# First pair's tokens turned by their gather, final norm weights by products, another order in the tail: a decoder layer on one core

## The chip, the cores and the metric

The kernel runs on one core of a Trainium2 chip. Its engines run side by side and meet at semaphores: PE (TensorE, matrix products into PSUM; PEld is its weight load), DVE (VectorE), ACT (ScalarE), POOL (GpSimd) and SP (SyncE, which here issues transfers to the 16 DMA engines). The metric is the device time of one execution in microseconds (us). Before the change, three runs gave 929.28 to 930.95 us with a median of 929.9 us.

## The reference, cut to what matters

One decoder layer on 512 tokens of 1024 numbers, in float32: a mixer of two kinds of attention, a residual, a two-level mixture of 32 experts, a residual, a final norm.

```python
def rms_norm(x, g):
    y = xf * lax.rsqrt(jnp.mean(xf * xf, axis=-1, keepdims=True) + EPS)
    return (y * g).astype(x.dtype)
...
    combine = jnp.einsum('tk,tke->te', w, jax.nn.one_hot(expert_id, MOE_N_EXPERTS, dtype=f32))
    for e in range(MOE_N_EXPERTS):
        hdn = jax.nn.silu(vt @ w_gate[e]) * (vt @ w_up[e])
        y = y + (combine[:, e:e + 1].astype(hdn.dtype) * hdn) @ w_down[e]
...
        h = h + hybrid_mixer(u, positions, w_in[layer], ...)
        h = h + hier_moe(rms_norm(h, g_ffn[layer]), w_grp[layer], b_grp[layer], w_exp[layer], b_exp[layer],
                         w_gate[layer], w_up[layer], w_down[layer])
    return rms_norm(h, g_final)
```

Each token goes to two of the 32 experts. An expert has three matrices of 2 MB each, so that all experts together hold 201 MB of weights, and all of them are read.

## The kernel before

The first half of the program (to about 447 us) is the mixer. Then comes the routing, and from about 452 us the experts, in 16 pairs. An expert has room for 64 of its tokens, so a pair fills 128 rows (a branch behind L1610 deals with experts that got more).

**The expert loop (L1407).** For each pair the rows of its tokens are gathered (`gather_rows`, an indirect DMA from `hs`, the copy of the layer's rows in DRAM), turned by eight transposes on PE into one PSUM tile named `y` (`turn_rows`, L1341), and scaled by the norm's gain into `xa` or `xb` (`turned`, L1346). `up_proj` (L1434) multiplies them with the gate weights (tile `g`) and the up weights (tile `u`), in eight steps k of 128 input columns. SiLU and a product with `u` follow (tile `pkM`, L1463 and L1465), four transposes (L1474), the down products into `y` (L1489), the scaling by the router's weight as a high and a low part (`scaled`, L1394 and L1395), and `combine` (L1389, L1390): one-hot products that scatter the pair's rows back to the tokens, and additions into `h`. `combine` of a pair runs between the gate and up products of the next one, in two halves of 512 columns.

**The weight ring (L1056 to L1076).** 22 tiles of 1 MB hold weights that are loaded ahead. `weights()` takes pieces in order; `refill()` starts as many loads as pieces were used up. In `up_proj` that is after the fourth and after the eighth step k, two pieces of 1 MB each. SP issues the loads in program order, and at most eight are under way.

**The first pair.** It does not gather by DMA, since its rows are still in `h`. `first_rows` multiplies the one-hot matrix `oh` (128 slots) with `h` (L1354, eight products of 512 columns, in float32) to get the rows, `rows_in` holds them, and `turn_rows` turns them. `oh` is built by DVE in `one_hot` (L1309), and right behind it DVE computes the remaining ranks (L1304) and their maximum `cmax` (L1318). Then `slots_of` finds the slots' weights and indices (L1365, `cw`, `idx`), and `gather_rows(1)` fetches the next pair's rows.

**The tail (L1502 on).** The last pair's down products are made in three column groups, `TAIL` = 512, 256 and 256 columns (`down`, L1531). Each group is scaled (`high` on ACT, `low` on DVE), scattered (`spread_out`, L1550: for each of four token tiles the high product, then the low one), added to `h` (`add_of`, L1557), and the squares of the sums are taken (`square`, L1561, in halves of 512 columns). `scale_of` makes 1/rms on POOL (L1521, L1522), `scaled_out` multiplies and stores (L1565 to L1567). `gfin`, the final norm's gain repeated over 128 partitions, is loaded by DMA (L1441).

**What sets the order.** On PE, SP, ACT and DVE the loop's order is that of the code, mostly (`manual_schedule`); before the loop a scheduler decides. The framework places the waits: for a PSUM tile it tracks the tile as a whole.

Of the kernel before, what the change touches and what calls it, by code (L numbers as in the profile page):

```python
# [11 lines left out]
F32 = mybir.dt.float32  # L12
# [9 lines left out]
P = 128  # L22
T = 512
# [24 lines left out]
def _w_in_columns():  # L48
# [13 lines left out]
_PACKS = {  # L62
    "E": [("gmix", 8), ("ident", 128), ("slot", 64), ("gff8", 8), ("none", 8), ("invf", 32), ("rowmask", 2), ("posv", 16), ("posk", 16),
# [19 lines left out]
def build(tc, A, dbg=None):  # L83
# [1222 lines left out]
    def one_hot(quad):  # L1306
        oh = wst.tile([P, NT, 4, CAP], F32R, name="raw2")
        for t in range(NT):
            tt(oh[:, t], slot[:, None, :].to_broadcast([P, 4, CAP]),  # L1309
               val[:, t, 4 * quad:4 * quad + 4][:, :, None].to_broadcast([P, 4, CAP]), op=OP.is_equal)  # L1310
        return oh
# [32 lines left out]
    def turned(pair, tp):  # L1344
        for ks in ((slice(0, 4), slice(4, 8)) if pair == 0 else (slice(0, 8),)):
            nc.vector.tensor_tensor(xs[pair][:, ks], tp[:, ks], cst("gff8")[:, ks, None].to_broadcast([P, ks.stop - ks.start, P]), op=OP.mult)  # L1346

    def first_rows():

        for half in range(2):  # L1350
            cs = slice(half * 512, half * 512 + 512)
            ps = pp.tile([P, 512], F32, name="cT"[half], bufs=2)
            for t in range(NT):
                mm(ps, fl2(oh[:, t, :2]).bitcast(F32), h[t][:, cs], start=t == 0, stop=t == NT - 1)  # L1354
            if half == 0:
                nc.scalar.activation(rows_in[:, cs], ps, AF.Copy)
            else:
                nc.vector.tensor_copy(rows_in[:, 512:768], ps[:, :256])
                nc.scalar.activation(rows_in[:, 768:], ps[:, 256:], AF.Copy)

# [40 lines left out]
    acc = h  # L1401
    rows_in = wst.tile([P, D], F32, name="raw0")
    before = None
    slots, xs = {}, {}
    ab, halves = {}, {}
    loads.enter_context(tc.manual_schedule(engines={E.PE}))
    for pair in range(NE // 2):  # L1407
        last = pair == NE // 2 - 1

        def rest_of(pcw, py, pyh, pair=pair, last=last):  # L1410

            combine(pyh, 0)
# [10 lines left out]
            spread(pair)  # L1423

# [13 lines left out]
        order = ExitStack()  # L1438
        if pair == NE // 2 - 2:
            gfin = wst.tile([P, D], F32, name="raw2")  # L1440
            nc.sync.dma_start(gfin, A["gfin"])  # L1441
        if pair == 0:
            order.enter_context(tc.manual_schedule(engines={E.Activation, E.DVE}))
        if pair == 0:
            first_rows()
            turned(0, turn_rows(0))
            slots_of(0)
            slots_of(1)
            gather_rows(1)
            for tag, k in [("g", k) for k in range(0, KD, 2)] + [("u", k) for k in range(0, KD, 2)]:  # L1450
                up_proj(tag, (k, k + 1))
                if (tag, k) == ("u", 4):
# [9 lines left out]
        sl = wk.tile([P, FF], F32, name="pkM")  # L1462
        nc.scalar.activation(sl, ab[pair, "g"], AF.Silu, scale=cw[:, 1:2])  # L1463
        if not last:
            tt(sl, sl, ab[pair, "u"], op=OP.mult)  # L1465
            up_proj("g", range(4), pair + 1)
        else:
            for _ in between:
                pass
            order.close()  # L1470
        if not last:
            tp = pp.tile([P, 4, P], F32, name="T", bufs=2)
# [29 lines left out]
        else:  # L1502
            hdT = wk.tile([P, 4, P], F32, name="xb")
            for j in range(4):
                tt(sl[:, j::4], sl[:, j::4], ab[pair, "u"][:, j::4], op=OP.mult)
                tp = pp.tile([P, P], F32, name="Tc"[j % 2], bufs=2)
                nc.tensor.transpose(tp, sl[:, j::4], ident)
                if j % 2:
                    nc.scalar.activation(hdT[:, j], tp, AF.Copy)
                else:  # L1510
                    nc.vector.tensor_copy(hdT[:, j], tp)

            ss3 = wk.tile([P, NT, 3], F32, name="ss3")
            nc.vector.memset(ss3[:, :, 1:2], EPS)
# [4 lines left out]
            def scale_of(t):  # L1519
                ts = slice(t, t + 1)  # L1520
                nc.gpsimd.tensor_tensor(rs3[:, 0, ts], rs3[:, 0, ts], ss3[:, t, 2:], op=OP.add)  # L1521
                nc.gpsimd.tensor_tensor(rs3[:, 1, ts], rs3[:, 0, ts], nhalf[:, ts], op=OP.pow)  # L1522
                return rs3[:, 1, ts]
# [17 lines left out]
            def spread_out(i, tags, per):  # L1541

                c0, n = TAIL[i]
                o = slice(c0 % 512, c0 % 512 + n)
                out = []
                for t in range(NT):
                    if t % per == 0:
                        ps = pp.tile([P, per, n], F32, name=tags[t], **({} if tags[t] in "guy" else dict(bufs=2)))
                    for v, y in enumerate((yhi, ylo)):
                        mm(ps[:, t % per], ohs[:, t].bitcast(y.dtype), y[:, o], start=v == t % per == 0,  # L1550
                           stop=v == 1 and t % per == per - 1, skip_group_check=True)
                    out.append(ps[:, t % per])
# [6 lines left out]
            def square(t, half):  # L1559
                jk = wk.tile([P, 512], F32, name="pkM")  # L1560
                nc.scalar.activation(jk, acc[t][:, 512 * half:512 * half + 512], AF.Square, scale=ROOT,  # L1561
                                     accum_out=ss3[:, t, 2 * half:2 * half + 1])

# [4 lines left out]

            loads.enter_context(tc.manual_schedule(engines={E.Activation, E.DVE}))
            high, low = down(0)  # L1570
# [39 lines left out]
    with tc.If(nmax > CAP):  # L1610
# [44 lines left out]
        for t in range(NT):  # L1655
            nc.vector.tensor_tensor(gh[t], acc[t], gfin, op=OP.mult)
            nc.scalar.activation(acc[t], acc[t], AF.Square, scale=ROOT, accum_out=ss3[:, t, 2:])
# [7 lines left out]
def pack(inputs):  # L1665
# [37 lines left out]
    put("gff8", f("g_ffn")[0].reshape(P, KD))  # L1703
    put("gffT", f("g_ffn")[0].reshape(KD, P).T)
    put("br", np.repeat(np.concatenate([f("b_grp")[0], f("b_exp")[0]])[None], P, 0))
    i = np.arange(P)
# [22 lines left out]
    for n in ("w_gate", "w_up", "w_down"):  # L1729
        d[n] = f(n)[0]  # L1730
    d["gfin"] = np.repeat(f("g_final")[None], P, 0)
    return d
# [13 lines left out]
```

## Time and profile before

| | us |
|---|---|
| median of three runs | 929.9 (929.28 to 930.95) |
| the profiled execution | 930.93 |
| its span, first to last instruction | 929.1 |
| around the span | 1.8 |

| engine | busy, us | share of the span |
|---|---|---|
| PE | 890.2 | 96% |
| PEld | 569.5 | 61% |
| DVE | 469.0 | 50% |
| ACT | 252.6 | 27% |
| POOL | 99.4 | 11% |

PE's share is an average over stages with different limits. From 500 to 890 us the DMA engines are full as well, and it is the waits at the end of that stretch, and what ran dry at its start, that tell which of the two sets the time. The mean granted clock was 0.988 of full speed.

### The profile page before, as it was taken

To read this page: it belongs to the slowest core of one execution; us is meant where nothing else is said; L and a number is where in the kernel's file an instruction comes from. 1 tells how busy PE (TensorE), PEld (TensorE's weight loads), DVE (VectorE), ACT (ScalarE), POOL (GpSimd) and SP (SyncE) were. 2 spreads that over 40 slices of the span, in tenths; PEclk is the share of its full clock that TensorE was granted. 3 is DMA by queue.
4 is the path that set the end of the run, shared out by engine and by line. 5 is a ranking of instruction groups with operands and counts; after the bars stand their busy time and mean duration, and the time that the engine had idled before them with its cause. 6 is when DMAs were issued, how large, how long until landed. Compare 5 with 4: busy or idle time off the path is not lost. (4 is left out here: it accounts for less than half of the span.)

```text
span 929.1 us, 12699 instructions
## 1 busy us (share of the span) xinstructions
PE 890.2 (96%) x4908; PEld 569.5 (61%) x4908; DVE 469.0 (50%) x1047; ACT 252.6 (27%) x539; POOL 99.4 (11%) x139
## 2 busy tenths in 40 slices
PE   8997999999999999999899999999999999999994
PEld 5877997899878777899534443444444334333432
DVE  5669664485877776644514433334343324322334
ACT  6542443245545555343101011001011100010014
POOL 0304000032111121500100000000000000000003
PEclk9997999999999999999999999999999999999997
DMA  8821222212111121995889999999999999999992
GB/s 320 315 90 46 91 86 65 77 54 66 49 46 46 47 80 53 416 419 188 317 357 419 419 418 420 419 419 420 419 418 420 419 418 421 418 420 418 421 381 109
DMA packets 47712, 251.89 MB, mean 271 GB/s; under 512 B 6114, under 2 KB 9442, under 8 KB 22688
## 3 DMA queue, kind: packets, MB, share of 16 engines
q1 hardware_dynamic: 45488, 247.10, 66.8%
q0 software_dynamic: 2160, 3.93, 1.1%
q8 instruction: 41, 0.67, 0.3%
q14 instruction: 23, 0.19, 0.1%
HBM read 250.23 MB, written 4.19 MB: 274 GB/s over the span
## 5 line engine op out<-in xcount | busy, mean ns | idle before, releaser
L1390 DVE TENSOR_TENSOR h<-h,c 128x512 f32<-128x512 f32 x60 | 38.6, 684 | 85.5 <-PE c L1389 85.5
L1395 DVE SCALAR_TENSOR_TENSOR hdT<-y,cw,raw 128x512 fp32r<-128x512 f32 x30 | 22.4, 748 | 103.9 <-ACT raw L1394 103.9
L1489 PE MATMUL y<-a,pkM 128*64 128x512 f32 x240 | 67.5, 597 | 1.9 <-DVE pkM L1476 1.4
L196 PE MATMUL z<-uhi,whi 128*128 128x512 f32 x160 | 66.8, 418 | 0.0
L185 PE MATMUL z<-whi,uhi 128*128 128x256 f32 x224 | 65.5, 292 | 0.2 <-ACT s L463 0.2
L1394 ACT ACTIVATE raw<-y,cw 128x512 fp32r<-128x512 f32 x30 | 20.6, 687 | 160.0 <-PE y L1489 108.4
L198 PE MATMUL z<-ulo,whi 128*128 128x512 f32 x160 | 63.4, 396 | 0.0
L187 PE MATMUL z<-whi,ulo 128*128 128x256 f32 x224 | 63.3, 283 | 0.0
L186 PE MATMUL z<-wlo,uhi 128*128 128x256 f32 x224 | 63.3, 283 | 0.0
L197 PE MATMUL z<-uhi,wlo 128*128 128x512 f32 x160 | 63.2, 395 | 0.0
L1477 ACT ACTIVATE pkM<-T 128x256 f32<-128x256 f32 x15 | 5.8, 384 | 204.9 <-DVE pkM L1476 204.9
L1332 POOL DMA_INDIRECT raw<-hs,idx x15 | 15.2, 1012 | 379.4 <-DVE idx L1376 197.1
L143 DVE TENSOR_TENSOR wlo<-raw,whi 128x1024 fp32r<-128x1024 f32 (+1 forms) x46 | 47.5, 1058 | 12.9 <-ACT whi L142 12.8
L142 ACT ACTIVATE whi<-raw 128x1024 fp32r<-128x1024 f32 (+1 forms) x48 | 41.6, 909 | 24.8 <-PE z L198 12.8
L1489 PE MATMUL y<-s,pkM 128*64 128x512 f32 x120 | 46.9, 596 | 0.7 <-DVE pkM L1476 0.7
L185 PEld LDWEIGHTS z<-whi,uhi 128*128 128x128 f32 x224 | 42.4, 189 | 0.5 <-ACT s L463 0.4
L186 PEld LDWEIGHTS z<-wlo,uhi 128*128 128x128 f32 x224 | 42.4, 189 | 0.2
L187 PEld LDWEIGHTS z<-whi,ulo 128*128 128x128 f32 x224 | 42.3, 189 | 0.0
L1489 PEld LDWEIGHTS y<-a,pkM 128*64 128x64 f32 x240 | 20.0, 137 | 36.3 <-issue 30.3
L871 ACT ACTIVATE pr<-S,st 128x512 f32<-128x512 f32 (+3 forms) x64 | 33.4, 524 | 31.6 <-DVE st L869 30.5
L1434 PE MATMUL g<-a,xa 128*64 128x512 f32 x136 | 38.2, 596 | 1.8 <-DMA a<-in_w_gate 1.8
L1390 DVE TENSOR_TENSOR h<-h,T 128x512 f32<-128x512 f32 x60 | 38.4, 681 | 0.0
(455 smaller groups left out, 2110.2 us busy)
## 6 DMA issues: line engine op xcount, KB each, us to landing
a<-in_w_down SPq DMA_DIRECT2D x31, 1024.0 KB, 19.9
a<-in_w_gate SPq DMA_DIRECT2D x29, 1024.0 KB, 20.3
a<-in_w_up SPq DMA_DIRECT2D x28, 1024.0 KB, 20.2
s<-in_w_up SPq DMA_DIRECT2D x18, 1024.0 KB, 20.5
s<-in_w_down SPq DMA_DIRECT2D x16, 1024.0 KB, 20.5
s<-in_w_gate SPq DMA_DIRECT2D x16, 1024.0 KB, 20.5
raw<-in_w_in SPq DMA_DIRECT2D x26, 512.0 KB, 4.6
b<-in_w_gate SPq DMA_DIRECT2D x8, 1024.0 KB, 20.4
```

Source lines behind the costliest of these rows:

```text
L142: nc.scalar.activation(hi, src, AF.Copy)
L143: lo_engine.tensor_tensor(lo, src, hi.bitcast(F32), op=OP.subtract)
L185: mm(ps[:, i], uhi[:, k, ts], hi[:, k], start=k == 0, stop=False)
L186: mm(ps[:, i], uhi[:, k, ts], lo[:, k], start=False, stop=False)
L187: mm(ps[:, i], ulo[:, k, ts], hi[:, k], start=False, stop=k == KD - 1)
L196: mm(ps, hi[:, k, cs], uhi[:, k], start=k == 0, stop=False)
L197: mm(ps, lo[:, k, cs], uhi[:, k], start=False, stop=False)
L198: mm(ps, hi[:, k, cs], ulo[:, k], start=False, stop=k == KD - 1)
L871: nc.scalar.activation(pr[:, j], sc[:, j], AF.Exp, scale=-1.0, bias=one_of(0, j), accum_out=one_of(1, j))
L1390: tt(acc[t][:, cs], acc[t][:, cs], ps, op=OP.add)
L1434: mm(ps[rows[i]], xs[pair][:, k, i * CAP:i * CAP + CAP], w[i][:, k % 4], start=k == 0, stop=k == KD - 1)
L1489: mm(y[rows[i], hs_], hdT[:, j, rows[i]], w[i][:, j % 2, hs_], start=j == 0, stop=j == 3)
```

## The change

Four things are changed, in one diff (tile and function names as above).

1. The first pair's tokens are computed turned: `first_tokens` takes 128 columns of `h` as the stationary operand and the one-hot matrix as the moving one, so that for each k four products (L1359 of the changed program) give the 128 columns of `xs[0]` at once. Eight such blocks fill one PSUM tile `y`; ACT evicts the even ones, DVE the odd ones, each with the gain. They stand between the gate products: three blocks, gate k 0 and 1, two blocks, gate k 2 and 3, two blocks, gate k 4 and 5, one block, the slots' products, gate k 6 and 7. `rows_in` is only zeroed ahead, by POOL. `one_hot` for the first four columns of pairs goes column by column.
2. `gfin` comes from eight small products in pair 14 (L1438, the gain as a column broadcast over 128 columns, times the identity) and two ACT copies; the DMA is gone.
3. In the last pair the second half of pair 14's `combine` moves from between the up products to around the transposes (`rest_of_before`, `add_before`), and the four transposes go into one PSUM tile, each evicted by ACT.
4. `spread_out` makes all high products, then all low ones; the squares are taken by `TAIL` group (512, 256, 256 columns), and the reduction over them stands behind the additions.

```diff
+    rows_in = wst.tile([P, D], F32, name="raw0")
+    nc.gpsimd.memset(rows_in, 0.0)
...
-        for t in range(NT):
-            tt(oh[:, t], slot[:, None, :].to_broadcast([P, 4, CAP]), ...
+        for c in ((0, 1), (1, 2), (2, 4)) if quad == 0 else ((0, 4),):
+            for t in ((0, 2), (2, 4)) if c[1] > 2 else ((0, 4),):
...
-    def first_rows():
...
+    def first_tokens(ks):
+
+        if 0 in ks:
+            xs[0] = wk.tile([P, KD, P], F32, name="xa")
+            first["y"] = pp.tile([P, KD, P], F32, name="y")
+        tp = first["y"]
+        for k in ks:
             for t in range(NT):
-                mm(ps, fl2(oh[:, t, :2]).bitcast(F32), h[t][:, cs], start=t == 0, stop=t == NT - 1)
...
+                mm(tp[:, k], h[t][:, k::KD], fl2(oh[:, t, :2]).bitcast(F32), start=t == 0, stop=t == NT - 1)
+            g = cst("gff8")[:, k:k + 1]
+            if k % 2:
+                nc.vector.tensor_scalar(xs[0][:, k], tp[:, k], g, None, op0=OP.mult)
             else:
...
+                nc.scalar.activation(xs[0][:, k], tp[:, k], AF.Copy, scale=g)
...
             yield
+            if last:
+                for _ in range(3):
+                    yield
+                late.update(yh=pyh)
+                return
             combine(pyh, 512)
...
+                if pair == NE // 2 - 2:
+                    yield
+                    gfin = wst.tile([P, D], F32, name="raw2")
+                    for half in range(2):
+                        ps = pp.tile([P, 4, P], F32, name="c", bufs=2)
+                        for j in range(4):
+                            mm(ps[:, j], cst("gfT")[:, 4 * half + j:4 * half + j + 1].to_broadcast([P, P]), ident, start=True, stop=True)
+                        nc.scalar.activation(gfin[:, half * 512:half * 512 + 512], ps.rearrange("p j c -> p (j c)"), AF.Copy)
...
-        if pair == NE // 2 - 2:
-            gfin = wst.tile([P, D], F32, name="raw2")
-            nc.sync.dma_start(gfin, A["gfin"])
...
-            first_rows()
-            turned(0, turn_rows(0))
+            first_tokens(range(3))
+            up_proj("g", (0, 1))
+            first_tokens((3, 4))
+            up_proj("g", (2, 3))
+            first_tokens((5, 6))
+            up_proj("g", (4, 5))
+            first_tokens((7,))
             slots_of(0)
             slots_of(1)
             gather_rows(1)
...
+            up_proj("g", (6, 7))
...
-                tp = pp.tile([P, P], F32, name="Tc"[j % 2], bufs=2)
-                nc.tensor.transpose(tp, sl[:, j::4], ident)
-                if j % 2:
-                    nc.scalar.activation(hdT[:, j], tp, AF.Copy)
-                else:
-                    nc.vector.tensor_copy(hdT[:, j], tp)
...
+            pa = [pp.tile([P, 512], F32, name="c", bufs=2) for _ in range(2)]
+            rest_of_before((0, 1), pa)
+            tp = pp.tile([P, 4, P], F32, name="T", bufs=2)
+            for j in range(4):
+                nc.tensor.transpose(tp[:, j], sl[:, j::4], ident)
+                nc.scalar.activation(hdT[:, j], tp[:, j], AF.Copy)
+            add_before((0, 1), pa)
+            pb = pp.tile([P, 2, 512], F32, name="y")
+            pb = [pb[:, i] for i in range(2)]
+            rest_of_before((2, 3), pb)
+            add_before((2, 3), pb)
+            spread(pair)
...
-                for t in range(NT):
...
+                for v, y in enumerate((yhi, ylo)):
+                    for t in range(NT):
...
-            red(rs3[:, 0], ss3[:, :, :2], axis=AX.X, op=OP.add)
             for t in range(NT):
                 add_of(1, t, p1[t])
+                square(t, 1)
             add_of(2, 0, p2[0])
-            square(0, 1)
             add_of(2, 1, p2[1])
-            square(1, 1)
+            square(0, 2)
+            red(rs3[:, 0], ss3[:, :, :3], axis=AX.X, op=OP.add)
+            square(1, 2)
...
-                    square(t + 2, 1)
+                    square(t + 2, 2)
```

How PE's instructions stand at the first pair, before (`oh` is `raw_4598`, its rows are `raw_4632`, `c` and `T` are the PSUM halves of the rows, `b_…` the first weight pieces):

```order
L1354 MATMUL c<-h,raw_4598 128x512 [waits DVE_49] x4
L1354 MATMUL T<-h,raw_4598 128x512 [waits Activation_49]
L1354 MATMUL T<-h,raw_4598 128x512 x3
L1341 MATMUL y<-keep,raw_4632 128x128 [waits Activation_49]
L1341 MATMUL y<-keep,raw_4632 128x128 x7
L1365 MATMUL c<-W_3868,raw_4598 128x8 [waits PE_49,Pool_49]
L1365 MATMUL c<-W_3868,raw_4598 128x8 x7
L1434 MATMUL g<-b_3908,xa 64x512 [waits DMAHW0_49,DVE_49]
L1434 MATMUL g<-b_3910,xa 64x512 [waits DMAHW1_49]
```

The same place now (`oh` is `raw_4600`; line numbers are those of the changed program, where L1451 is the gate and up product):

```order
L1359 MATMUL y<-raw_4600,h 128x128 [waits DVE_49,PE_49]
L1359 MATMUL y<-raw_4600,h 128x128 x3
L1359 MATMUL y<-raw_4600,h 128x128 [waits Activation_49]
L1359 MATMUL y<-raw_4600,h 128x128 x3
L1359 MATMUL y<-raw_4600,h 128x128 [waits DVE_49]
L1359 MATMUL y<-raw_4600,h 128x128 x3
L1451 MATMUL g<-b_3908,xa 64x512 [waits DMAHW0_49]
L1451 MATMUL g<-b_3910,xa 64x512 [waits DMAHW1_49]
```

What moved: the rows' products, the transposes and the gate products were three runs one behind the other; now each block of four products begins with a wait for the engine that evicts the block before it, and gate products come after the third block. The first wait on DVE is for the count that the reduction `cmax` brings, behind all of `one_hot` and the remaining ranks; before, it was for the first of the four `one_hot` instructions.

Further on, PE in the changed program has the last block and the slots' products (L1370) here:

```order
L1359 MATMUL y<-raw_4600,h 128x128 [waits Activation_49]
L1359 MATMUL y<-raw_4600,h 128x128 x3
L1370 MATMUL c<-W_3868,raw_4600 128x8 [waits Pool_49]
L1370 MATMUL c<-W_3868,raw_4600 128x8 x7
L1451 MATMUL g<-a_3912,xa 64x512
L1451 MATMUL g<-a_3914,xa 64x512
L1451 MATMUL g<-a_3912,xa 64x512 [waits DVE_49]
L1451 MATMUL g<-a_3914,xa 64x512
```

What moved: the slots' products, on whose indices `gather_rows(1)` hangs, had all eight gate steps behind them and now have two. Their user on PE, the transposes of the second pair's rows (`turn_rows`), stands behind step k = 5 of the up products in both programs.

PE at the last pair's transposes, before (`pkM` holds the hidden rows, `xb` the turned ones; L1531 is the down product):

```order
L1507 MATMUL T<-keep,pkM 128x128 [waits DVE_49]
L1507 MATMUL c<-keep,pkM 128x128 [waits DVE_49]
L1531 MATMUL g<-s_3932,xb 64x512 [waits DMAHW0_49,DVE_49]
L1531 MATMUL g<-a_4143,xb 64x512 [waits DMAHW1_49]
```

And now (L1534 scatters pair 14's second half, `raw_4633` and `hdT` are its high and low parts; L1571 is the down product):

```order
L1534 MATMUL c<-raw_4633 128x512 [waits DVE_49,Activation_49]
L1534 MATMUL c<-hdT,raw_4633 128x512 [waits DVE_49]
L1544 MATMUL T<-keep,pkM 128x128 [waits DVE_49]
L1544 MATMUL T<-keep,pkM 128x128 [waits DVE_49,Activation_49] x3
L1534 MATMUL y<-raw_4633 128x512 [waits PE_49]
L1534 MATMUL y<-hdT,raw_4633 128x512
L1571 MATMUL g<-s_3932,xb 64x512 [waits DMAHW0_49,PE_49]
L1571 MATMUL g<-a_4143,xb 64x512 [waits DMAHW1_49]
```

What moved: eight scatter products that stood between the up products now stand four ahead of the transposes and four behind them, and the second to fourth transposes wait for ACT, which evicts the one before.

## Rows read from the trace of the kernel before

**Rows 1.** Stretches: busy us of PE, PEld, DVE, ACT, POOL; clock; DMA share; GB/s.
```profile
460.00:465.00 5.00, 4.14 (x26) 2.64 (x28) 2.75 (x12) 1.67 (x2) 0.00 (x0) 1.00 0.13 51
750.00:800.00 50.00, 46.86 (x212) 19.09 (x210) 15.14 (x34) 4.18 (x7) 1.98 (x2) 1.00 1.01 419
850.00:890.00 40.00, 36.56 (x153) 13.84 (x151) 9.77 (x16) 3.13 (x5) 0.00 (x0) 1.00 1.01 419
```

**Rows 2.** Timeline of SP: start, length, what (the first pair's refills).
```profile
466.49 0.81 SPq L1054 DMA_DIRECT2D b<-in_w_down  x2
469.93 0.96 SPq L1054 DMA_DIRECT2D a<-in_w_down  x2
478.03 0.80 SPq L1054 DMA_DIRECT2D a<-in_w_up  x2
```

**Rows 3.** Timeline of the first pair: start, length, engine, line, in brackets the wait.
```profile
452.73 3.70 PE L1354 MATMUL c<-h,raw 128*128 128x512 f32 x8 [0.72 <-DVE raw L1309]
454.05 0.18 DVE L1318 TENSOR_REDUCE cmax<-z 128x1 f32<-128x32 f32 x1
461.72 1.03 PE L1365 MATMUL c<-W,raw 128*128 128x8 f32 x8
462.81 3.65 PE L1434 MATMUL g<-b,xa 128*64 128x512 f32 x16
465.60 1.28 POOL L1332 DMA_INDIRECT raw<-hs,idx  x1 [11.23 <-DVE idx L1376]
469.73 5.32 PE L1434 MATMUL u<-a,xa 128*64 128x512 f32 x24
474.98 1.16 PE L1341 MATMUL y<-keep,raw 128*128 128x128 f32 x8
```

**Rows 4.** DMA issues: out<-in, operation, KB each, us to landing (at 465.60; at 876.65).
```profile
raw<-hs,idx POOLq DMA_INDIRECT x1, 7.7
...
s<-in_w_up SPq DMA_DIRECT2D x1, 1024.0 KB, 20.7
```

**Rows 5.** Prices: a timeline row (start, length), then a group (busy, mean ns).
```profile
145.89 1.99 PEld L520 LDWEIGHTS S<-qbd,lv 128*128 128x128 f32 x16
...
L1509 ACT ACTIVATE xb<-c 128x128 f32<-128x128 f32 x2 | 0.6, 278 | 9.9 <-PE c L1507 9.9
```

**Rows 6.** Stretches around the longest idle time of PE (columns as in rows 1).
```profile
78.00:79.00 1.00, 0.00 (x0) 0.00 (x0) 1.00 (x2) 0.48 (x1) 1.00 (x2) 0.61 0.00 0
...
82.00:88.00 6.00, 6.00 (x28) 6.00 (x29) 5.88 (x12) 0.18 (x1) 0.79 (x4) 0.50 0.00 0
```

**Rows 7.** Timeline of PE: around idle times (brackets), and 451.44 before the first pair.
```profile
76.21 0.27 PE L476 MATMUL T<-keep,rpa 64*128 64x64 f32 x1 [0.78 <-DVE rpa L446]
81.88 1.44 PE L491 MATMUL o<-pkG,lv 128*128 128x2 f32 x6 [5.40 <-POOL lv L488]
...
451.44 0.57 PE L1277 MATMUL z<-xb 128*128 128x128 f32 x4
...
795.58 0.65 PE L1434 MATMUL g<-a,xa 128*64 128x512 f32 x2 [1.76 <-DMA a<-in_w_gate]
```

**Rows 8.** Timeline of the last pair to its first down product; the reduction.
```profile
887.37 1.93 PE L1434 MATMUL g<-a,xb 128*64 128x512 f32 x6 [1.26 <-DMA a<-in_w_gate]
...
896.55 0.50 PE L1389 MATMUL c<-raw 128*128 128x512 f32 x1
...
898.57 0.64 PE L1434 MATMUL u<-wlo,xb 128*64 128x512 f32 x1
...
902.34 1.26 DVE L1505 TENSOR_TENSOR pkM<-pkM,u 128x128 f32<-128x128 f32 x4 [2.15 <-PE u L1434]
902.78 0.39 PE L1507 MATMUL T<-keep,pkM 128*128 128x128 f32 x1 [0.56 <-DVE pkM L1505]
...
903.98 0.64 PE L1531 MATMUL g<-s,xb 128*64 128x512 f32 x1
...
915.41 0.16 DVE L1587 TENSOR_REDUCE rs<-ss 128x4 f32<-128x8 f32 x1 [0.88 <-ACT pkM L1561]
```

More of the change, by code (lines that the diff above doesn't have):

```diff
@@ L1344, in turned @@
     def turned(pair, tp):
[L1345 to L1352 removed]
+        nc.vector.tensor_tensor(xs[pair], tp, cst("gff8")[:, :, None].to_broadcast([P, KD, P]), op=OP.mult)
+    def first_tokens(ks):
[4 more added lines that the diff above has]
+        for k in ks:
             for t in range(NT):
[L1354 to L1359 removed]
+                mm(tp[:, k], h[t][:, k::KD], fl2(oh[:, t, :2]).bitcast(F32), start=t == 0, stop=t == NT - 1)
+            g = cst("gff8")[:, k:k + 1]
+            if k % 2:
+                nc.vector.tensor_scalar(xs[0][:, k], tp[:, k], g, None, op0=OP.mult)
+            else:
+                nc.scalar.activation(xs[0][:, k], tp[:, k], AF.Copy, scale=g)
     def slots_of(pair):
@@ L1401, in build @@
     acc = h
[L1402 to L1405, printed above, removed]
+    before = gfin = None
+    slots, xs, first = {}, {}, {}
+    ab, halves, late = {}, {}, {}
     loads.enter_context(tc.manual_schedule(engines={E.PE}))
@@ L1410, in rest_of @@
         def rest_of(pcw, py, pyh, pair=pair, last=last):
+            nonlocal gfin
             combine(pyh, 0)
@@ L1449, in build @@
             gather_rows(1)
-            for tag, k in [("g", k) for k in range(0, KD, 2)] + [("u", k) for k in range(0, KD, 2)]:
-                up_proj(tag, (k, k + 1))
-                if (tag, k) == ("u", 4):
+            up_proj("g", (6, 7))
+            for k in range(0, KD, 2):
+                up_proj("u", (k, k + 1))
+                if k == 4:
                     turned(1, turn_rows(1))
@@ L1462, in build @@
         sl = wk.tile([P, FF], F32, name="pkM")
+        if last:
+            order.enter_context(tc.manual_schedule(engines={E.Activation}))
         nc.scalar.activation(sl, ab[pair, "g"], AF.Silu, scale=cw[:, 1:2])
@@ L1470, in build @@
             order.close()
+            loads.enter_context(tc.manual_schedule(engines={E.Activation, E.DVE}))
         if not last:
@@ L1505, in build, with rest_of_before, add_before @@
                 tt(sl[:, j::4], sl[:, j::4], ab[pair, "u"][:, j::4], op=OP.mult)
-                tp = pp.tile([P, P], F32, name="Tc"[j % 2], bufs=2)
-                nc.tensor.transpose(tp, sl[:, j::4], ident)
-                if j % 2:
-                    nc.scalar.activation(hdT[:, j], tp, AF.Copy)
-                else:
-                    nc.vector.tensor_copy(hdT[:, j], tp)
-            ss3 = wk.tile([P, NT, 3], F32, name="ss3")
+            def rest_of_before(ts, ps):
+                for t, p in zip(ts, ps):
+                    for v, y in enumerate(late["yh"]):
+                        mm(p, ohs[:, t].bitcast(y.dtype), y, start=v == 0, stop=v == 1)
+            def add_before(ts, ps):
+                for t, p in zip(ts, ps):
+                    tt(acc[t][:, 512:], acc[t][:, 512:], p, op=OP.add)
+            pa = [pp.tile([P, 512], F32, name="c", bufs=2) for _ in range(2)]
[10 more added lines that the diff above has]
+            spread(pair)
+            ss3 = wk.tile([P, NT, 4], F32, name="ss3")
             nc.vector.memset(ss3[:, :, 1:2], EPS)
@@ L1545, in spread_out @@
                 out = []
-                for t in range(NT):
[L1547 to L1550, printed above, removed]
+                for v, y in enumerate((yhi, ylo)):
+                    for t in range(NT):
+                        if v == 0 and t % per == 0:
+                            ps = pp.tile([P, per, n], F32, name=tags[t], **({} if tags[t] in "guy" else dict(bufs=2)))
+                        if v == 0:
+                            out.append(ps[:, t % per])
+                        mm(out[t], ohs[:, t].bitcast(y.dtype), y[:, o], start=v == t % per == 0,
                            stop=v == 1 and t % per == per - 1, skip_group_check=True)
-                    out.append(ps[:, t % per])
                 return out
@@ L1557, in add_of, with square @@
                 tt(acc[t][:, cs], acc[t][:, cs], ps, op=OP.add)
-            def square(t, half):
+            def square(t, i):
+                c0, n = TAIL[i]
                 jk = wk.tile([P, 512], F32, name="pkM")
-                nc.scalar.activation(jk, acc[t][:, 512 * half:512 * half + 512], AF.Square, scale=ROOT,
-                                     accum_out=ss3[:, t, 2 * half:2 * half + 1])
+                i += i > 0
+                nc.scalar.activation(jk[:, :n], acc[t][:, c0:c0 + n], AF.Square, scale=ROOT, accum_out=ss3[:, t, i:i + 1])
             def scaled_out(t, r):
@@ L1567, in scaled_out @@
                 nc.sync.dma_start(A["out"][t * P:(t + 1) * P, :], gh[t])
-            loads.enter_context(tc.manual_schedule(engines={E.Activation, E.DVE}))
             high, low = down(0)
@@ L1730, in pack @@
         d[n] = f(n)[0]
-    d["gfin"] = np.repeat(f("g_final")[None], P, 0)
     return d
```

13 lines of the change are left out of this document (7 added, 6 removed).

## The prediction

> **What bounds the kernel now.** I read the stretches of 50 us first. From 500 to 890 us the DMA engines are full at 419 GB/s, while PE is idle for 3.14 us of 750 to 800 and 3.44 us of 850 to 890 [rows 1]; what it waits for there is a gate weight, at 795.58 and last at 887.37 [rows 7, 8]. So the weight stream sets the end, PE has at least 6.6 us to spare against it, and behind 887.37 PE's own chain runs to the end. Next I asked when the stream last ran dry. From 460 to 465 the DMA share is 0.13 [rows 1]: the 22 tiles of the ring are full, and nothing can be loaded until the gate products use some up. The first refill is issued at 466.49, the next at 469.93, the fourth at 478.03 [rows 2]. A refill is 2 MB, which is 5.0 us at 419 GB/s, so each must follow the one before in the stream within 5.0 us, or the stream stands. Before, it never stands again: due times are 471.5, 476.5, 481.5, and all are met with 1.6 us or more. Hence the rule for the first pair: the moments at which its gate and up products free tiles are the clock of the whole loop, and what is late by more than its margin is lost for good.
>
> **The first pair's tokens.** Removed are eight products of 512 columns, about 0.9 us each (a float32 product leaves two records, eight of which take 3.70 us), and eight transposes, from 452.73 to 461.72; then slots 1.03 us and gates 6.92 us, 0.865 a step, follow [rows 3]. Added are 32 float32 products of 128x128. Sixteen weight loads, for eight such products, take 1.99 us [rows 5], so one costs 0.25 and a block of four 1.0 us. Two waits are new. The first block needs the count of `cmax`, ready at 454.23 [rows 3], so it starts at 454.3 instead of 452.73. And each block waits for the eviction of the block before it: an ACT eviction of 128x128 takes 0.278 us [rows 5], and the products' end and two handovers come on top. In [rows 8] a transposed tile's path, 902.78 to 903.98 for four, hides this, so it has no row of its own; bounds are 0.28 (the eviction alone) and 1.0, and I take 0.7, nearer to PE's wait of 0.56 behind a DVE step of about 0.3 [rows 8]. The wait shows before blocks 1, 2, 4 and 6; before 3, 5 and 7 gate products hide it.
>
> Refill 1 comes after five blocks, three waits and four gate steps: 454.3 + 5.0 + 2.1 + 3.46 + 0.2 to SP = 465.0, that is 1.5 earlier. Refill 2 comes after eight blocks, four waits, eight steps and the slots: 454.3 + 8.0 + 2.8 + 6.92 + 1.03 + 0.2 = 473.2, that is 3.3 later. It is due at 465.0 + 5.0 = 470.0, so the stream stands. Against the old due time of 471.5 the stream is late by **1.7 us** (0.3 to 3.0 with waits of 0.35 to 1.0).
>
> On these waits, the only evidence from rows is the eviction's 0.278 us; the framework makes PE wait for every block, the fifth too, which lies in another bank than the fourth. The Trainium skill ("PSUM — Partial Sum Buffer", "PSUM bank collisions raise a hardware error") says to guard PSUM by bank and quadrant, not by address, so that three of the four exposed waits are needed and the one before block 4 is not. No run here shows a collision; without that wait the sum would be 0.7 less.
>
> **The gather behind it.** The slots' products now have two gate steps behind them instead of eight. Before, they ended at 462.75, the gather was issued at 465.60 (2.85 later) [rows 3] and took 7.7 us to land [rows 4], at 473.3; PE asked for it at 474.98, after six up steps [rows 3], 1.7 to spare. After: slots end at 473.05 - 1.73 = 471.3, gather at 474.15, landed at 481.85. PE reaches the transposes at 473.05 + 5.25 = 478.3. **PE stands for 3.5 us.** This does not depend on the eviction waits, since both sides move together. Behind the transposes (1.1 us) stand up steps 6 and 7 (1.73 us), and refill 4 waits for these: 481.85 + 1.1 + 1.73 + 0.1 = 484.8. It is due at 473.2 + 10.0 = 483.2, so the stream loses another **1.6 us** at full clock.
>
> But PE's clock may not stay full. After 76.48, PE stood 5.40 us [rows 7]; the granted clock of 78 to 79 averages 0.61, so it fell to 1.2 GHz at about 78.2, 1.7 us into the idle time, and from 82 to 88 it was still 0.50 with PE fully busy [rows 6]. Idle times of 1.76 us at 795.58 [rows 7] left it at full clock (the mean there stays 1.00 [rows 1]). A stand of 3.5 us lies between, past the point at which it fell. I take it that it falls: then the transposes take about 2.0 and the two steps 3.46, refill 4 is issued at 487.4, and the loss is **4.2 us** instead of 1.6. Refills 5 and 6 then have margins of about 1 us and hold. PE is by then some 3.5 us further behind the stream than before, 6 with what follows below, inside its 6.6.
>
> **Edits at nothing.** The `gfin` products are eight of 0.25, 2 us of PE in pair 14, covered by the idle 3.44 us of 850 to 890; if that cover is gone, they cost 2. The missing 512 KB transfer stood behind weights that PE had waited for already: 0. The memset runs on POOL long before (0 to 0.8), the other `one_hot` order on DVE off the path. ACT's copies of `gfin` are off the path.
>
> **The tail.** The scatter of 896.55 to 898.57, 2.0 us, leaves the up products [rows 8]. The up piece behind it was issued at 876.65 and lands 20.7 us later [rows 4], at 897.3, so not all is gained: 0.7 to 2.0, I take 0.9. From the SiLU products' first product on DVE (902.34) to the first down product (903.98) it is 1.64 us [rows 8]. After, three transposes wait for ACT's eviction of the one before (0.7 each, 2.1 in all), and of the eight scatter products (0.25 each by 2.0 / 8) four stand behind the transposes, 1.0, and four ahead, mostly in the old wait of 0.56 [rows 8]: +2.9 (0.5 to 3.8). The end gains where the reduction waited 0.88 for a square on ACT [rows 8]; of it I take 0.5. Sum -0.9 + 2.9 - 0.5 = **+1.5** (-1.0 to +2.5).
>
> **Sum.** 1.7 + 4.2 + 1.5 = +7.4 on the profiled execution of 930.9 gives 938.3; the median lies 1.0 below the profiled one, so **937.2 us**.
>
> **The rivals.** (1) The clock stays full through the stand: 1.7 + 1.6 + 1.5 = +4.8, 934.7. For it: the stand whose rows show the fall was a longer one, with less work ahead of it. (2) The clock falls at the start as well. PE's last product before the blocks ends at 452.01 [rows 7], the first block starts at 454.3, 2.3 us later, past the 1.7. Then the first blocks and steps run at half, about 2.5 us more before refill 2: +9.9, 939.7. Against it: DVE's first wait may end earlier, and short products run until 452. (3) The eviction waits cost little and the clock falls at the gather: with waits of 0.2 the stream's first loss is 1.7 - 4 x 0.5 = -0.3, the tail 1.5 - 3 x 0.5 = 0, so with 4.2 it is +3.9, 933.8. (4) The other side, not slower: the handover through PSUM is fast. Seven waits are exposed, four in the first pair, three in the tail; each 0.1 us of them is 0.7 us of the time. At zero, refill 2 is issued at 470.4, ahead of the old due time by 1.1, refill 4 is late by 1.6 still and the tail is -0.6: -0.1, 929.8. From waits of 0.28 us on and at full clock the sum is within 0.2% (1.9 us), from zero on it would be a gain. For it: the eviction itself is only 0.278 us [rows 5]. Against it: PE's wait of 0.56 [rows 8] behind a shorter step. That the change does not do what it says (gather still in time) is excluded by the order alone: 1.73 + 5.25 of PE against 2.85 + 7.7.
>
> **How the numbers follow.** Forecast 0.42 (936 to 938.5); (1) 0.22; (2) 0.11; (3) 0.12; (4) 0.13 (928.5 to 931.7). The range leaves out most of (4) and a part of (2): 931.0 to 939.6. A difference of 0.2%, 1.9 us, is about what a measurement of this kernel can tell from no change. Slower by more: 0.83, all but (4). Same: 0.12, most of (4). Faster: 0.05, what is left of (4), with some help from the tail.
>
> **What will show it.** The first block at 454.3; PE gaps of 0.7 between blocks 0, 1, 2, before 4 and 6, with ACT or DVE as releaser; refills at 465.0 and 473.2 with the DMA share low between about 472 and 475; the gather issued near 474, PE idle some 3.5 us before the second pair's transposes with a DMA as releaser; a granted clock of 0.5 from about 480 to 488; refill 4 at 487 (485 if the clock stays) and DMA dry before it; PE's last wait for a gate weight near 893 instead of 887.37; in the tail four transposes 0.8 us apart. It is wrong if the gather lands in under 5 us, if the stream's rate after 500 us is above 420 GB/s, or if waits are near 0.3.

## The result and the profile after

The changed kernel takes 946.38 us (945.20 to 947.71), the kernel before in the same comparison 930.02: a ratio of 1.0176, with an interval of 1.0158 to 1.0193. That is 16.4 us slower. The forecast was 937.2 with a range of 931.0 to 939.6: the direction was right, the size was not. The profiled execution has a span of 944.5 us, 15.4 more than before.

PE at the first pair, timeline of the changed kernel (start, length, engine, line; L1359 is a block of the first tokens, L1451 a gate or up product, L1370 the slots, L1345 the second pair's transposes; in brackets the idle time and its releaser):

```profile
453.83 2.24 PE L1359 MATMUL y<-raw,h 128*128 128x128 f32 x8 [2.36 <-DVE cmax L1322]
456.66 2.27 PE L1359 MATMUL y<-raw,h 128*128 128x128 f32 x8 [0.59 <-ACT xa L1364]
459.45 2.27 PE L1359 MATMUL y<-raw,h 128*128 128x128 f32 x8 [0.52 <-DVE xa L1362]
461.65 3.13 PE L1451 MATMUL g<-b,xa 128*64 128x512 f32 x8
464.70 2.17 PE L1359 MATMUL y<-raw,h 128*128 128x128 f32 x8
...
480.79 1.03 PE L1370 MATMUL c<-W,raw 128*128 128x8 f32 x8
481.76 1.94 PE L1451 MATMUL g<-a,xa 128*64 128x512 f32 x8
483.52 5.32 PE L1451 MATMUL u<-a,xa 128*64 128x512 f32 x24
491.89 1.97 PE L1345 MATMUL y<-keep,raw 128*128 128x128 f32 x8 [3.05 <-DMA raw<-hs,idx]
```

Each row of eight records is one block of four products. The waits are there, 0.52 to 0.59 us, and so is the stand before the transposes, 3.05. What I had not seen coming is the second column: a block takes 2.2 us, not 1.0. Before, slots and gates followed at 461.72 and 462.81 and the up products at 469.73 [rows 3]; now the up products begin at 483.52.

SP's refills, timeline of the changed kernel, which answer to [rows 2]:

```profile
471.47 0.81 SPq L1054 DMA_DIRECT2D b<-in_w_down  x2
483.72 0.80 SPq L1054 DMA_DIRECT2D a<-in_w_down  x2
487.15 1.08 SPq L1054 DMA_DIRECT2D a<-in_w_gate  x2
496.24 3.76 SPq L1054 DMA_DIRECT2D a<-in_w_up  x3
```

Refill 2 is issued at 483.72. The stream of before would have wanted it at 471.5, so 12.2 us are lost; refill 4 is due 10 us later, at 493.7, and comes at 496.24, which is another 2.5. Together that is 14.7, an estimate from two rows. How late the stream then is shows at a weight that PE waits for in both kernels, first before, then now (timelines of PE, each in its own kernel):

```profile
856.72 0.64 PE L1434 MATMUL g<-s,xa 128*64 128x512 f32 x1 [1.61 <-DMA s<-in_w_gate]
```

```profile
871.06 0.64 PE L1451 MATMUL g<-s,xa 128*64 128x512 f32 x1 [1.60 <-DMA s<-in_w_gate]
```

That is 14.3 us later: of the 14.7 next to nothing has come back in the 370 us between, in which the DMA engines run at 418 to 420 GB/s, as before (419 to 420).

Stretches of the changed kernel (columns as in [rows 1]) with the clock and, in the last column, the GB/s:

```profile
453.00:454.00 1.00, 0.17 (x1) 0.20 (x1) 0.83 (x4) 0.00 (x0) 0.82 (x3) 0.92 0.99 221
454.00:455.00 1.00, 1.00 (x5) 1.00 (x6) 0.00 (x0) 0.00 (x0) 0.00 (x0) 0.50 0.80 303
465.00:466.00 1.00, 1.00 (x6) 1.00 (x6) 0.00 (x0) 0.00 (x0) 0.00 (x0) 1.00 0.00 0
475.00:476.00 1.00, 1.00 (x6) 1.00 (x5) 0.00 (x0) 0.00 (x0) 0.00 (x0) 0.50 0.97 401
491.00:492.00 1.00, 0.11 (x1) 0.11 (x2) 0.00 (x0) 0.00 (x0) 0.00 (x0) 0.70 1.03 426
492.00:493.00 1.00, 1.00 (x5) 1.00 (x6) 0.00 (x0) 0.00 (x0) 0.00 (x0) 0.50 1.01 426
494.00:495.00 1.00, 1.00 (x4) 0.28 (x4) 1.00 (x1) 0.00 (x0) 0.00 (x0) 0.60 1.02 426
```

The clock fell to 1.2 GHz three times: at the end of the stand of 2.36 us before the first block (at about 453.84, worked out from the mean of 0.92), in the middle of the blocks, and in the stand of 3.05 us before the transposes (at about 491.4, from the mean of 0.70). The row of 465 to 466 shows the stream standing: nothing is loaded until refill 1.

The last pair, timeline of the changed kernel, answering to [rows 8] (L1528 is the SiLU product, L1544 the transposes, L1571 the down product):

```profile
915.23 1.26 DVE L1528 TENSOR_TENSOR pkM<-pkM,u 128x128 f32<-128x128 f32 x4 [7.97 <-PE u L1451]
916.72 0.39 PE L1544 MATMUL T<-keep,pkM 128*128 128x128 f32 x1 [0.37 <-ACT xb L1545]
917.47 0.39 PE L1544 MATMUL T<-keep,pkM 128*128 128x128 f32 x1 [0.37 <-ACT xb L1545]
918.23 0.39 PE L1544 MATMUL T<-keep,pkM 128*128 128x128 f32 x1 [0.37 <-ACT xb L1545]
919.46 0.64 PE L1571 MATMUL g<-s,xb 128*64 128x512 f32 x1
```

From 915.23 to 919.46 it is 4.2 us where it was 1.6 [rows 8], 2.6 more. The SiLU products themselves come 12.9 us later than before (902.34), 1.4 less than the 14.3 of the stream. Between the two places the scatter among the up products has gone, PE's last wait for a weight (1.26 at 887.37 [rows 8]) has gone, and the gain's products have come in; these rows do not separate the three. The tail with them is worth about +1.1 to +1.2: the span is 15.4 longer.

### The profile page after: what moved, and what is told of

It is laid out like the page before. It is cut to its first block, busy times and chain, and to the rows that moved or that the text cites. A ratio compares the mean times of both kernels' runs of the same rounds, so it can differ in the third digit from the quotient of the medians.

```text
span 944.5 us, 12822 instructions
## 1 busy us (share of the span) xinstructions
PE 903.3 (96%) x4964; PEld 584.2 (62%) x4964; DVE 467.0 (49%) x1032; ACT 256.1 (27%) x553; POOL 100.1 (11%) x140
## 4 chain that ended last, share of the span: by engine, by line
PE 64%; DMA 25%; DVE 5%; issue 3%; ACT 1%; POOL 1%; SPq 0%; POOLq 0%; DVEq 0%; ACTq 0%
PE u L1451 6%; PE g L1451 6%; PE y L1512 5%; DMA a<-in_w_up 5%; DMA s<-in_w_gate 4%; DMA a<-in_w_gate 4%; PE z L196 4%; PE z L198 4%; PE z L197 4%; PE z L185 3%; PE z L187 3%; PE z L186 3%; DMA s<-in_w_down 2%; DMA whi<-in_w_down 2%; DMA wlo<-in_w_up 2%
## 5 line engine op out<-in xcount | busy, mean ns | idle before, releaser
L1451 PE MATMUL g<-a,xa 128*64 128x512 f32 x136 | 39.0, 608 | 0.0
L1197 PE MATMUL z<-whi,s 128*128 128x256 f32 x128 | 37.3, 291 | 0.0
```

What stands on the lines that cost most here:

```text
L1197: mm(ps, mhi, w[:, 0, k], start=t % 2 == 0 and kh == 0 and k == 0, stop=False, skip_group_check=True)
L1451: mm(ps[rows[i]], xs[pair][:, k, i * CAP:i * CAP + CAP], w[i][:, k % 4], start=k == 0, stop=k == KD - 1)
```

## The experiments

My theory after this reading: the products' price was wrong, because `h[t][:, k::KD]` reads every eighth number of a row as the stationary operand, and the price that I had taken for a product was of an operand that lies together. A rival: a float32 product of 128 columns with `h` as the stationary operand is that slow in any case. Beside it stood three smaller causes that overlap: the waits with the clock that they cost, the gather, and the tail.

**The step of the stationary operand.** Steps 1, 2, 4 and 8 in one program:

```diff
-                mm(tp[:, k], h[t][:, k::KD], fl2(oh[:, t, :2]).bitcast(F32), start=t == 0, stop=t == NT - 1)
+                sd = (1, 1, 2, 2, 4, 4, 8, 8)[k]
+                mm(tp[:, k], h[t][:, k:k + P * sd - sd + 1:sd] if sd < 8 else h[t][:, k::KD], ...
```

> The first pair's blocks read their stationary operand with a step of 1 column in blocks 0 and 1, of 2 in 2 and 3, of 4 in 4 and 5, and of 8, as in the changed kernel, in 6 and 7 (in 0 to 5 these are other columns of h than the layer needs, so the first pair's tokens are not the reference's here; the number of products is the same). Theory S, that the step makes the weight load long: the weight loads fall from 0.33 us to about 0.19 with step 1 (as where one-hot columns that lie together were loaded, 0.19), and a block at full clock takes 1.0 us instead of 2.2, with steps of 2 and 4 somewhere between or as long as 8. Theory F, that a float32 product of 128 columns with h as the stationary operand is that long whatever the step: 0.33 us and 2.2 us in every block.

The time of that one run was 944.25 us. The weight loads on PEld (timeline, eight loads to a block), blocks 0, 3, 4 and 7:

```profile
454.00 0.97 PEld L1360 LDWEIGHTS y<-raw,h 128*128 128x128 f32 x8 [2.43 <-issue]
463.14 1.03 PEld L1360 LDWEIGHTS y<-raw,h 128*128 128x128 f32 x8 [0.81 <-issue]
464.88 1.94 PEld L1360 LDWEIGHTS y<-raw,h 128*128 128x128 f32 x8 [0.71 <-DVE xa L1363]
476.63 1.99 PEld L1360 LDWEIGHTS y<-raw,h 128*128 128x128 f32 x8 [0.95 <-issue]
```

At full clock eight loads take 0.97 us with step 1, 1.03 with step 2, 1.94 with step 4 and 1.99 with step 8. Theory S holds for these products, and it has an edge: two float32 numbers apart costs nearly nothing, four apart costs as much as eight. (The transposes are an exception; see the last section.) The Trainium skill ("SBUF — State Buffer", in the section "Door 1: The DMA port swizzle (why `[64,N]` ≈ `[32,N]`)") says that SBUF is read in lines of 16 bytes and that at least two accesses must fall in a line for full rate. Steps of 8, 16 and 32 bytes bear that out: two, one and one numbers to a line, and 1.03, 1.94 and 1.99 us; the transposes, with 32 bytes and 0.97 us, do not. The next sentence there calls a step of four float32 numbers free, and for these loads it is not: 1.94 us.

**Neighbouring columns in every block.** The same kernel as the changed one but for `h[t][:, k * P:k * P + P]`.

> As the changed kernel, but every block reads 128 columns of h that lie together (other columns than the layer needs, so the first pair's tokens are not the reference's; nothing is left out). Theory S: blocks at full clock take 1.0 us, the three at half clock about 2.0; refill 2 comes some 6 us earlier, near 478 instead of 483.7, and the time falls to 939 to 941 us. Theory F: no change, 946.4.

It takes 940.26 us, a ratio of 1.0107 (1.0087 to 1.0126) where the changed kernel had 1.0176: 6.1 us less by the medians, 6.9 if each kernel is set against the kernel before in its own comparison, so the step is worth 6 to 7 us. Timeline of its PE, the third and the fourth block, and of SP, the second refill:

```profile
458.62 2.08 PE L1359 MATMUL y<-raw,h 128*128 128x128 f32 x8 [0.52 <-DVE xa L1362]
463.43 1.16 PE L1359 MATMUL y<-raw,h 128*128 128x128 f32 x8
476.53 0.80 SPq L1054 DMA_DIRECT2D a<-in_w_down  x2
```

A block at full clock takes 1.16 us by its row. At half clock it still took 2.08 (blocks 1 and 2) against 2.27 with the step, so the step's full price, 1.0 us a block, is paid in those blocks alone that run at full clock. The fall of the clock in the middle of the blocks is absent from this execution, and the gate steps are the shorter for it; that is a part of the 6 to 7 us.

**The gather ahead of the blocks.** `slots_of(0)`, `slots_of(1)` and `gather_rows(1)` stand in front of `first_tokens(range(3))`, the rest is the changed kernel.

> As the changed kernel, but the slots' products and the second pair's gather stand ahead of the first block. If the stand of PE before the second pair's transposes (3.05 us here) costs the stream what refill 4 is late, 496.24 against a due time of 493.7, it falls by 2.5 us to 943.9, with refill 2 still near 483.7. If that stand is covered by the ring, no change, 946.4.

It takes 943.88 us, a ratio of 1.0153 (1.0129 to 1.0177), 2.5 us less than the changed kernel by the medians, 3.3 if each is set against the kernel before in its own comparison. The two intervals overlap, so the time alone would not settle it; the trace does. Timelines of PE and SP:

```profile
487.73 1.16 PE L1345 MATMUL y<-keep,raw 128*128 128x128 f32 x8
490.78 3.76 SPq L1054 DMA_DIRECT2D a<-in_w_up  x3
```

The transposes have no wait any more and run at full clock, and refill 4 is issued 8.1 us after refill 2 (482.67), inside the 10 us that two refills last, where the changed kernel needs 12.5. Refill 2 itself is 1.05 earlier here; the clock did not fall in the middle of the blocks in this execution, so the gather's own part is the 2.5.

**The first pair undone.** The kernel before, with the new tail and the gain by products alone.

```diff
-            first_tokens(range(3))
-            up_proj("g", (0, 1))
...
+            first_rows()
+            turned(0, turn_rows(0))
+            slots_of(0)
+            slots_of(1)
+            gather_rows(1)
```

> The first pair as in the kernel before (rows, transposes, slots, gates); the final norm's gain by products and the new tail are kept. By the trace the end of the up products gained 1.4 us on the stream and the way from there to the first down product lost 2.6: 930.0 + 1.1 = 931.1. If the tail and the gain's products were free, 930.0; if what PE lost in pair 14 to them counts in full, 933.

It takes 931.98 us against 930.80, a ratio of 1.0012 (1.0002 to 1.0022): the tail and the gain cost 1.2 us, as read, with an interval of 0.2 to 2.0. Fifteen of the sixteen us are the first pair's.

**A PSUM tile for each block.** The waits of the first pair's blocks go without taking a wait away: each block writes its own tile.

```diff
-            first["y"] = pp.tile([P, KD, P], F32, name="y")
-        tp = first["y"]
         for k in ks:
+            tp = pp.tile([P, P], F32, name="cT"[k % 2], bufs=2)
...
```

> As the changed kernel, but each block of the first pair's tokens has a PSUM tile of its own, from the four of the names c and T in turn, so that no block waits for the eviction of the one before it, and none for the reader of the PSUM that lay under tile y (the reduction cmax). If these waits and the fall of the clock that they bring are a part of the loss by their sizes in the trace (start 1.3 us, four waits of 0.5 to 0.6, gate products at half clock 1.9 us), refill 2 comes some 5 us earlier, at 478 to 479, blocks still take 2.2 us, and the time is 941. If only the weight loads' step matters, nothing moves: 946.4.

It takes 940.43 us, a ratio of 1.0105 (1.0090 to 1.0120): the waits and what hung on them were worth 6 us by the medians, 6.9 by each kernel's own comparison. Its PE and SP (timelines):

```profile
452.41 2.27 PE L1358 MATMUL c<-raw,h 128*128 128x128 f32 x8 [1.12 <-DVE raw L1313]
454.48 2.10 PE L1358 MATMUL T<-raw,h 128*128 128x128 f32 x8
456.38 2.01 PE L1358 MATMUL c<-raw,h 128*128 128x128 f32 x8
458.32 1.94 PE L1450 MATMUL g<-b,xa 128*64 128x512 f32 x8
476.84 0.80 SPq L1054 DMA_DIRECT2D a<-in_w_down  x2
```

The first block starts on the first one-hot columns, not behind `cmax`: the wait for `cmax` had come with tile `y`, which lay on the PSUM that `cmax` reads. Blocks follow one another without a wait, and the first gate steps run at full clock (1.94, in the changed kernel 3.13), though the first blocks still do not (0.55 in 454 to 455). Refill 2 comes 6.9 us earlier.

**All three at once, made whole.** Neighbouring columns, own tiles, slots behind the third block. Block k then gives the numbers 128k to 128k + 127 of the tokens, so the first pair's gate and up weights are loaded in that row order too, in lines of 2 KB:

```diff
-                    v = A[n][e].rearrange("(p k) f -> p k f", p=P)
+                    v = A[n][e].rearrange("(k p) f -> p k f" if p == 0 and n != "w_down" else "(p k) f -> p k f", p=P)
```

> The changed kernel with three things mended at once: the stationary operand lies together (128 neighbouring columns of h; the first pair's gate and up weights are loaded with the matching rows, so that the sums are the same), each block has its own PSUM tile, and the slots' products with the gather stand behind the third block. If step, waits, clock and gather are all of the first pair's loss, refill 2 comes near 469.6 (452.9 + 8 blocks of 1.0 + 6.9 + 1.0 + 0.2), 1.9 us ahead of the old due time of 471.5, and only the tail's 1.1 us is left: 930.8 - 1.9 + 1.1 = 930.0. If something else of the new order costs, or if refill 1 or a later one sets the stream, above 932.

It takes 931.21 us against 930.97, a ratio of 1.0005 (0.9996 to 1.0014): no difference that can be measured, and 15 us less than the changed kernel. It lies 1.2 above what was expected, and why is not settled. In its profiled execution the clock fell at the first blocks, though PE had stood for 1.11 us only, and refill 2 came at 471.93 instead of 469.6.

**The same first pair, old tail.**

> The kernel before with the first pair of the run above (blocks of neighbouring columns, own PSUM tiles, slots behind the third block), and nothing else changed: no new tail, the final gain by DMA. Expected 930.8 - 1.9 = 928.9; if the first pair's earlier refills are worth nothing, 930.8.

It takes 929.18 us against 930.97, a ratio of 0.9981 (0.9972 to 0.9990): 1.8 us faster than the kernel before, and the fastest of all. Its SP (timeline), a weight that PE waits for and a stretch of it; then the same stretch of the run above, where the clock fell:

```profile
463.34 0.81 SPq L1054 DMA_DIRECT2D b<-in_w_down  x2
470.15 0.80 SPq L1054 DMA_DIRECT2D a<-in_w_down  x2
...
854.92 0.64 PE L1437 MATMUL g<-s,xa 128*64 128x512 f32 x1 [1.60 <-DMA s<-in_w_gate]
...
454.00:456.00 2.00, 2.00 (x20) 2.00 (x19) 1.09 (x5) 0.37 (x1) 0.83 (x3) 1.00 0.86 233
```

```profile
454.00:456.00 2.00, 2.00 (x12) 2.00 (x12) 1.01 (x5) 0.37 (x1) 1.00 (x3) 0.55 0.88 240
```

Refill 1 is issued at 463.34, 3.2 us earlier than before, and refill 2 follows at 470.15, 6.8 later, so only part of that is kept: 470.15 against the due 471.5 is 1.35 earlier. PE's products ahead of the blocks began 0.47 later in this execution (451.91 against 451.44 in [rows 7]), so counted from there it is 1.8. The weight that PE waits for at 856.72 before comes at 854.92, 1.8 earlier as well, and so is the time that the runs show.

**The tail's transposes in two tiles.** As the run with the first pair undone, but the last pair's transposes use two PSUM tiles in turn and DVE and ACT evict in turn.

```diff
-            tp = pp.tile([P, 4, P], F32, name="T", bufs=2)
             for j in range(4):
-                nc.tensor.transpose(tp[:, j], sl[:, j::4], ident)
-                nc.scalar.activation(hdT[:, j], tp[:, j], AF.Copy)
+                tp = pp.tile([P, P], F32, name="T", bufs=2)
+                nc.tensor.transpose(tp, sl[:, j::4], ident)
+                if j % 2:
+                    nc.scalar.activation(hdT[:, j], tp, AF.Copy)
+                else:
+                    nc.vector.tensor_copy(hdT[:, j], tp)
```

> The first pair as in the kernel before, the new tail, but with the last pair's transposes in two PSUM tiles in turn, evicted by DVE and ACT in turn as before. The three exposed evictions cost 0.46 us each in the trace of the changed kernel (transposes 0.76 apart instead of 0.30); with them gone the tail should lose about 1.2 us less: 930.8 + 1.1 - 1.2 = 930.7 against 932.0 with one tile. If the scatter products around the transposes are what costs, no change against 932.0.

It takes 930.39 us against 930.97, a ratio of 0.9999 (0.9990 to 1.0007), where one tile gave 1.0012. The last SiLU products on DVE, transposes on PE and the first down product (timelines), first with one tile (the run with the first pair undone), then with two:

```profile
902.19 1.25 DVE L1518 TENSOR_TENSOR pkM<-pkM,u 128x128 f32<-128x128 f32 x4 [7.98 <-PE u L1447]
903.75 0.39 PE L1534 MATMUL T<-keep,pkM 128*128 128x128 f32 x1 [0.43 <-ACT xb L1535]
...
906.50 0.64 PE L1561 MATMUL g<-s,xb 128*64 128x512 f32 x1
```

```profile
900.24 1.26 DVE L1518 TENSOR_TENSOR pkM<-pkM,u 128x128 f32<-128x128 f32 x4 [8.00 <-PE u L1447]
901.10 0.39 PE L1534 MATMUL T<-keep,pkM 128*128 128x128 f32 x2
901.76 0.54 PE L1534 MATMUL T<-keep,pkM 128*128 128x128 f32 x2 [0.27 <-DVE xb L1538]
903.15 0.64 PE L1564 MATMUL g<-s,xb 128*64 128x512 f32 x1
```

One exposed wait of 0.27 is left of three of 0.37 to 0.43, and from the SiLU products (900.24) to the down product it is 2.9 us instead of 4.3 (902.19 to 906.50). The intervals of the two runs touch (1.0002 to 1.0007 lies in both), so by the times alone it is not settled; by the trace the exposed evictions were the tail's loss. With them gone no difference from the kernel before can be measured, so the scatter products' new place gains about as much as it costs.

## Where the prediction failed, by its own steps

- **What bounds the kernel: held.** The first pair's refills set the end, and what they are late stays lost: refills 2 and 4 were late by 12.2 + 2.5 = 14.7 us, and the stream was 14.3 late 370 us on.
- **The price of a product: this is the step that failed.** "Sixteen weight loads, for eight such products, take 1.99 us [rows 5], so one costs 0.25" took a row whose operand lies together for an operand read in steps of 32 bytes. The block measured 2.2 us, not 1.0: the eight rows add up to 17.8 us against 8.0, +9.8 (+9.3 where the rows' overlap is taken off). With neighbouring columns the eight rows add up to 11.1, so 6.7 of the 9.8 are the step's; the rest is the half clock of blocks 1 and 2, at which they take 2.08 with neighbouring columns too, and a block's own 1.16 instead of 1.0. The step stood in the diff (`k::KD`), and I gave this term one value and no bounds, while I gave bounds to terms of a tenth of its size. With the row of [rows 5] as the lower end and nothing known above, the range should have been open upwards.
- **The waits: held.** 0.52 to 0.59 us against 0.7, at the four places named. By the rule of the Trainium skill ("PSUM — Partial Sum Buffer", "PSUM bank collisions raise a hardware error") that I weighed there, the wait before block 4 would not be needed; it was there, since the framework tracks the tile as a whole, and its 0.52 was paid. No run took that one wait away by itself.
- **Refills 1 and 2:** 465.0 and 473.2 forecast, 471.47 and 483.72 measured. Of the 10.5 us on refill 2, counted from the start of each row to the next without the waits, the blocks are 9.3 and the gate steps, some at half clock, 2.3; shorter waits (0.65) and a start 0.5 earlier go the other way. So the stream's first loss, 1.7 in the sum, was 12.2.
- **The gather: held in kind.** PE stood 3.05 us against 3.5, with the gather as releaser, because the slots' products moved behind six gate steps. The two parts were off in opposite ways: the gather was issued 1.3 us behind the slots' products (483.09) instead of 2.85, and took 8.8 us to land instead of 7.7. The clock fell in that stand, as the likeliest case had it, but came back some 3 us after PE had started again (0.60 in 494 to 495), so refill 4 was late by 2.5 and not by 4.2. I had put the fall at 1.7 us into an idle time, from one row; here it came about 2.4 and 2.6 us after PE's last product.
- **The clock at the start:** rival (2), given 0.11, came true beside the forecast: the clock fell at about 453.9. I had treated it and the fall at the gather as cases; both happened, and a third that I had not named, at about 474.
- **The tail: held in sum.** +1.5 forecast, +1.2 measured by undoing the rest. By the trace its terms were -1.4, +2.6 and about -0.1 where I had -0.9, +2.9 and -0.5. (The waits and products named for the +2.9 already come to 3.1; what was taken off them the prediction does not say.)
- **Edits at nothing:** the last weight wait is now that at 871.06, and the one of 1.26 at 887.37 [rows 8], forecast for 893, is gone: with the first pair undone 0.42 of it is left (888.43), so the gain's products and the tail use up most of it. That these products cost nothing was not tried alone; with the tail they cost 1.2.
- **The rivals:** none had a block at twice its price. The rival on the other side, (4), fell with the waits at 0.52, and with it the cheap evictions of (3). (All rivals but (4), with the forecast, add up to 0.87; the prediction has 0.83 for slower.)

Without the blocks' 9.3 us the rest comes to about 6.5, not far from the forecast's 7.4, but that is luck: the gate steps' 2.3 was not in the sum, and the gather (-1.7), the waits (-0.65), the start (-0.5) and the tail (-0.4) were all smaller than forecast.

The single changes do not simply add up. By the medians the step is worth 6.1, the tiles 6.0, the gather 2.5 and the tail 1.2, 15.8 of 16.4; with each kernel set against the kernel before in its own comparison they are 6.9, 6.9, 3.3 and 1.2, 18.3 in all. The parts overlap: the step costs little where the clock is low, and each of the three runs on the first pair also had a higher mean granted clock (0.982, 0.986, 0.985 in its profiled execution) than the changed kernel (0.981).

## What to carry to other kernels

A price taken from a row may hold for that row's access pattern alone: before an operation is costed, compare the steps of its operands with those of the row, and where no row has the step, leave the upper end open. Where a full stream of weights sets the time, look for the moments at which it can run dry, and count what stands ahead of them; here blocks at twice their price and what hung on them came out as 15 us at the end of the program, 450 us later. A tile tracked as a whole turns eight independent blocks into a chain, and here four tiles in turn took the chain away.

## What was not expected of the hardware

- Weight loads of 128 float32 columns: eight take 0.97 us with step 1, 1.03 with step 2, 1.94 with step 4, 1.99 with step 8, at full clock. At half clock step 1 takes 1.78, so there the step of 8 (1.98) is nearly free. Timelines of PEld at half clock, block 1 with neighbouring columns (the run with the four steps), then block 1 of the changed kernel:

```profile
455.76 1.78 PEld L1360 LDWEIGHTS y<-raw,h 128*128 128x128 f32 x8 [0.78 <-ACT xa L1365]
```

```profile
456.66 1.98 PEld L1359 LDWEIGHTS y<-raw,h 128*128 128x128 f32 x8 [0.89 <-ACT xa L1364]
```

- The transposes read `rows_in` with the same step of eight and are not slowed: eight took 1.16 us [rows 3], their eight weight loads 0.97. So the step alone does not make a load long; why the transposes are spared was not tried.
- The same instructions at the same place ran at full clock in one profiled execution (1.00 in 454 to 456) and at half in another (0.55), after the same idle time of 1.11 us. In the changed kernel the clock fell at about 474.3 behind waits of no more than 0.52 us, with PE busy in between. After the stand of 2.36 us before the first block it fell at that stand's end, at about 453.84; with neighbouring columns, after a stand of 2.37 us, the first block still ran at full clock (1.13 us) and the fall came at about 455.7. What decides it these runs do not show.
- The gather of the second pair's rows, 7.7 us from issue to landing before, took 8.8 in the changed kernel, but 4.2 with the gather ahead of the blocks (issued 9 us before refill 1) and 4.1 with all three at once. A latency read from one row was not fixed either.
